# Program order for half 1's first product, a block sum behind two low parts, output-block differences in place, and the last bank in two halves

## The chip, the cores and the metric

The kernel runs on one core of one Trainium2 chip. The metric is the device time of the whole program in microseconds, the median over the runs shown. Engines are named as the profile names them: PE is TensorE's matmul stream, PEld its weight loads, DVE is VectorE, ACT is ScalarE, POOL is GpSimd and SP is SyncE, which here only issues DMAs.

## What is computed

One hybrid encoder layer on 1024 tokens of width 1024, in float32:

```
mod = silu(c) @ w_ada + b_ada;  sh1, sc1, gt1, sh2, sc2, gt2 = split(mod, 6)
h = rmsnorm(x, norm1_g) * (1 + sc1) + sh1
u, v, q, k, va, gate_a, gate_b = split(h @ w_in)
a_out = gmlp_branch(u, v, ...) @ w_a
b_out = window_attention_branch(q, k, va, ...) @ w_b
x = x + gt1 * ((sigmoid(gate_a) * a_out + sigmoid(gate_b) * b_out) @ w_o)
h2 = rmsnorm(x, norm2_g) * (1 + sc2) + sh2
f_gate, f_up = split(h2 @ w_ffn_in)              # two times 1024 x 2816
x = x + gt2 * ((silu(f_gate) * f_up) @ w_ffn_out)
```

## The kernel before

**Precision and units.** Every float32 matrix is used as a rounded high part and a low part (value minus high part), and every product is three matmuls: high by high, high by low, low by high. A *unit* is a 128x1024 piece of a weight: `unit` (line 157) takes its raw load (SP queue, tag `raw`, three buffers), a cast on ACT for the high part (tag `wh`, three buffers) and a subtraction on DVE, or on POOL, for the low part (tag `wl`, three buffers).

**Halves.** `half(hf)` (line 747) does the first sub-layer's projections and both branches for 512 tokens, first for half 0, then for half 1. Its first product is the loop `for k in range(KT)`, line 897: eight steps, and in each step the 128 rows k of h meet the q weights (four 512-wide outputs) and the k/v weights (in half 1, three 256-wide outputs). A q unit serves two steps and a k/v unit four. In half 1 the loop also emits, at steps 1, 3 and 5, the unit of the q weights for the next two steps; at step 3 the raw load of the second k/v unit and at step 4 that unit; after steps 2 and 3 the loads of two columns of `w_ada` (`ada_half_load`, tags `hs` and `xs`, two buffers each); after steps 4 and 5 the two dot products on DVE of a column loaded earlier (`ada_half`), followed by the loads of another column into the same two buffers; after steps 6 and 7 only the dot products. The v product (`v_product`, line 1004) follows, with units of `w_v`.

**What sets the order.** Instructions of one engine run in the order of its queue. A planner writes that order from its own estimate of when inputs are ready, except where an instruction is pinned. With `in_order[0]` set, each instruction of DVE, ACT, POOL and PE is queued behind the instruction emitted before it on its engine. Loads through `load` (line 137) are always pinned so on SP. Half 0's first product runs with `in_order` set and half 1's does not. `after(ins, prev)` (line 143) pins one instruction behind one other. The second sub-layer runs under a manual schedule: program order throughout.

**Block sums.** From the end of half 1 on, products are done as seven-product (Strassen-like) block products, which need sums of blocks. `block_load(k, "b1")` (line 596) makes one of their inputs, the sum of the high and low part of a block of half 1's h, on POOL. At the same time POOL subtracts the low parts of the units of `w_ab` for the branch projections (`prepare`, line 1020, called with POOL by default).

**The FFN.** For each of 22 feature tiles f there are seven steps i of 12 matmuls (`product`, `evict`). Two neighbouring tiles make a pair e = f // 2, whose four 512-wide results are the blocks b0 to b3 of one tile `o` of the pool `mid` (eight buffers). `hidden_sums` (line 1681) stores `o` to `tA[e]` by a POOL DMA and queues four DVE operations in the list `later`, one of which is run at each step: d0 = b0-b1, d1 = -d0-b3, d2 = b3-b1, d3 = -d1-b2. They are written to a second `mid` tile `n`, which is stored to `tB[e]`. The first one is queued at step 3 of the pair's second tile, the other three at that tile's step 6. `load_out` and `out_sums` use `mid` too (`wo`), with a store to `wS`. The blocks of T3 and T4 and the sums `ws` hold five of the eight buffers.

**The output product.** 77 work items (seven products by eleven pairs) of 12 matmuls each run from `wS`, `tA`, `tB` and `w_out` (`step_mm`, line 2018). The last two items are done together, one 512-wide bank d of four after another; `finish` scales a bank on DVE, adds it into `acc` and stores it by an SP DMA.

Of the kernel before, what the change touches and what calls it, by code (L numbers as in the profile page):

```python
# [8 lines left out]
F32 = mybir.dt.float32  # L9
# [3 lines left out]
ALU = mybir.AluOpType  # L13
# [3 lines left out]
P = 128  # L17
# [3 lines left out]
HALF = 512  # L21
# [17 lines left out]
def kernel(  # L39
# [25 lines left out]
    in_order = [False]  # L65
# [18 lines left out]
    V, A, G, T = (Engine(e) for e in (nc.vector, nc.scalar, nc.gpsimd, nc.tensor))  # L84
# [16 lines left out]
    def nm(s):  # L101
        n_names[0] += 1
        return f"{s}_{n_names[0]}"
# [48 lines left out]
    def raw_unit(src):  # L152
        r = wpool.tile([P, UNIT], F32, tag="raw", name=nm("raw"))
        load(r, src)
        return r

    def unit(src, eng=None, raw=None):
        r = raw if raw is not None else raw_unit(src)
        h = wpool.tile([P, UNIT], F32R, tag="wh", name=nm("wh"))
        l = wpool.tile([P, UNIT], F32R, tag="wl", name=nm("wl"))  # L160
        A.copy(h, r)
        (eng or V).tensor_tensor(l, r, h.bitcast(F32), op=ALU.subtract)
        return h, l

    def mm3(out, a, b, first, last):
# [73 lines left out]
    NP = NF // 2  # L239
# [351 lines left out]
    nsh, g1b = nshb[:, :8], nshb[:, 8:]  # L591
    blk = {}

    chunk, kinds = {}, []

    def block_load(k, name):
        if k < 4:
            if name == "b1":
                chunk[name] = stream("xs")
                G.tensor_tensor(chunk[name], *(x[:, k, :].bitcast(F32) for x in blk["B22"]), op=ALU.add)  # L600
                return
            chunk[name] = stream("hs" if name[0] == "a" else "xs")
            store(chunk[name], (x0d if name[0] == "a" else x1sd)[4 * int(name[1]) + k])
# [143 lines left out]
    def half(hf):  # L747
# [142 lines left out]
        def halo_product(k):  # L890
            w = kv_unit(k // 4)
            ok = slice(k % 4 * 256, k % 4 * 256 + 256)
            for a, b in ((k, 0), (k, 1), (KT + k, 0)):
                T.matmul(kps[NT], hl4[:, a, :], w[b][:, ok], start=k + b == 0 and a == 0,
                         stop=a == 2 * KT - 1)

        for k in range(KT):
            if hf == 0:
                x = xt[k]
# [120 lines left out]
        def prepare(eng=G):  # L1020
            if srcs:
                units.append(unit(srcs.pop(0), eng))

        def begin_unit():
            r = raw_unit(srcs.pop(0))
# [518 lines left out]
    def pool_dma(dst, src):  # L1544
        nc.gpsimd.dma_start(dst, src)

    def dma(dst, src):
        nc.sync.dma_start(dst, src)
# [127 lines left out]
            if later:  # L1676
                later.pop(0)()

    first_sum = {}

    def hidden_sums(f):

        e, t = divmod(f, 2)
        if t == 0:
            hidden[e].append(mid.tile([P, 2048], F32, tag="mid", name=nm("hid")))
        o, n = hidden[e]
        b = [o[:, i * Q : (i + 1) * Q] for i in range(4)]
        d = [n[:, i * Q : (i + 1) * Q] for i in range(4)]
        if t == 0:
            first_sum[e] = lambda: V.tensor_tensor(d[0], b[0], b[1], op=ALU.subtract)  # L1690
            return
        pool_dma(tA[e], o)
        later.append(lambda: V.scalar_tensor_tensor(out=d[1], in0=d[0], scalar=-1.0, in1=b[3],
                                                    op0=ALU.mult, op1=ALU.subtract))
        later.append(lambda: V.tensor_tensor(d[2], b[3], b[1], op=ALU.subtract))
        later.append(lambda: (V.scalar_tensor_tensor(out=d[3], in0=d[1], scalar=-1.0, in1=b[2],
                                                     op0=ALU.mult, op1=ALU.subtract),
                              pool_dma(tB[e], n)))

    wo_raw = {}  # L1700

# [103 lines left out]
    def out_row(e, t, d):  # L1805
        return w_out[2 * e + t][:, d * Q : (d + 1) * Q]

    def blk(x, i):
        return lambda e: x[e][:, i * Q : (i + 1) * Q]
# [2 lines left out]
    OUT = (  # L1812
        (lambda e: out_row(e, 0, 0), blk(tA, 0), 1, True),
        (lambda e: out_row(e, 1, 0), blk(tA, 2), 1, False),
        (blk(wS, 1), blk(tB, 2), 0, True),
        (lambda e: out_row(e, 1, 1), blk(tB, 3), 0, False),
        (blk(wS, 3), blk(tB, 0), 1, True),
        (blk(wS, 0), blk(tB, 1), 1, False),
        (blk(wS, 2), blk(tA, 3), 1, False),
    )  # L1820
    work = [(i, e) for i in range(7) for e in range(NP)]
# [14 lines left out]
    def split_step(n):  # L1836
        if n < len(work):
            if n % 5 < 3:
                ready[n] = wtiles()
            else:  # L1840
                ready[n] = [outp[0].tile([P, UNIT], F32R, tag=f"o{x}", name=nm(f"o{x}"), bufs=2)
                            for x in "hl"]
            split2(raws[n], *ready[n])
# [9 lines left out]
    with tc.manual_schedule():  # L1853
# [46 lines left out]
        for f, i in steps:  # L1900
            product(f, i)
            if chain:
                run_chain(2 if (f, i) < (0, 5) else 0)
            u = place[f, STEPS[i][0]]
            copies = f and i in (0, 2, 3) or f < 2 and i in (4, 5)
            if copies:
                evict(f, i)
            prepare(u + 2, 1)
            if chain:
                run_chain(2 if (f, i) != (0, 5) else 0)  # L1910
            if i == 6 or f < EARLY:
                prepare(u + 2, 1)
            if not copies:
                evict(f, i)
            if (f, i) == (0, 5):
                evict(0, 6)
            if i == 3 and f % 2:
                later.append(first_sum.pop(f // 2))
            if i == 6 or (f, i) == (0, 5):
                hidden_sums(f)  # L1920
            elif f > 2:
                run_later(1)
            if f >= EARLY:
                e, p = divmod(7 * (f - EARLY) + i, 10)
                if e < NP and p == 0:
                    load_out(e)
                if e < NP and p == 5:
                    later.extend(lambda e=e, p=p: out_sums(e, p) for p in range(4))
            if (f, i) == (NF - 3, 0):
                again.extend(stream("hs") for _ in range(2))  # L1930
                for j in range(2):
                    dma(again[j], silu_d[:, j * 512 : (j + 1) * 512])
            if (f, i) == (NF - 2, 6):
                row_load(0)
            if f == NF - 1 and i in (3, 5):
                split_step(i // 2 - 1)
# [16 lines left out]
        def put(q, hf, d):  # L1953
            (dma if (q, hf) == (0, 1) else pool_dma)(
                outT[(4 * q + d) * P : (4 * q + d + 1) * P, hf * HALF : (hf + 1) * HALF],
                acc[q][hf][:, d, :])

        def finish(i, d, bank):
            gt = mod[:, GT2 + d : GT2 + d + 1]
            if i == 0:  # L1960
                A.copy(c1[:, d, :], bank)
            elif i == 1:
                o = acc[0][0][:, d, :]
                V.scalar_tensor_tensor(out=o, in0=bank, scalar=gt, in1=o, op0=ALU.mult, op1=ALU.add)
                put(0, 0, d)
            elif i == 2:
                V.tensor_tensor(e7[:, d, :], bank, c1[:, d, :], op=ALU.add)
            elif i == 3:
                V.tensor_tensor(e4[:, d, :], bank, c1[:, d, :], op=ALU.add)
            elif i == 4:  # L1970
                V.tensor_tensor(e4[:, d, :], e4[:, d, :], bank, op=ALU.subtract)
            elif i == 5:
                last5[d] = tmp()
                A.copy(last5[d], bank)
            else:
                o = acc[0][1][:, d, :]
                V.scalar_tensor_tensor(out=o, in0=bank, scalar=gt, in1=o, op0=ALU.mult, op1=ALU.add)
                put(0, 1, d)
# [36 lines left out]
            if n == 54:  # L2015
                V.tensor_scalar(ngt, mod[:, GT2 + 4 : GT2 + 8], -1.0, None, op0=ALU.mult)

        def step_mm(n, d):
            i, e = work[n]
            _, _, b, first = OUT[i]  # L2020
            w = ready[n]
            ds, ts = slice(d * P, (d + 1) * P), slice(Q, 2 * Q)
            for j, (p, q) in enumerate(((0, 0), (0, 1), (1, 0))):
                T.matmul(sets[b][d], w[p][:, ds], w[q][:, ts], start=first and e + j == 0,
                         stop=e == NP - 1 and j == 2, skip_group_check=True)

        sets = {}
        for n, (i, e) in enumerate(work):
            _, _, b, first = OUT[i]
            if e == 0 and first:  # L2030
                sets[b] = [at_bank() if b else mm_bank() for _ in range(4)]
            last = n == len(work) - 1
            if n < len(work) - 2:
                for d in range(4):
                    step_mm(n, d)
            elif last:
                for d in range(4):
                    for m in (n - 1, n):
                        step_mm(m, d)
            if e == NP - 1:  # L2040
                for d in range(4):
                    finish(i, d, sets[b][d])
            split_step(n + 4)
            fetch(n + 12)
            gain_dots(n)
            if n in (8, 24, 40, 52):
                m = (8, 24, 40, 52).index(n)
                load_acc(m // 2, m % 2)
            if e < 4:
                finish_rest(i - 1, e)  # L2050
            if i == 6 and 4 <= e < 8:
                second_row(e - 4)
# [68 lines left out]
```

## Time and profile before

| | us |
|---|---|
| median of 3 runs | 1237.61 |
| lowest and highest run | 1235.74, 1238.73 |
| the profiled execution's own time | 1236.14 |
| its span, first to last instruction | 1234.4 |
| PE busy within the span | 1225.4 (99%) |
| DVE, ACT, POOL busy | 907.8, 582.6, 181.0 |

Matmul ends are modelled, so PE's busy time contains pipelined overlap, and a short stall can hide in it: the start-to-start distance of neighbouring matmuls is the better measure. All engine instructions carry line 77, since a wrapper records them, so groups are told apart by tile names. A wait is put down to the one releaser that came last.

### The profile page before, as it was taken

To read this page: it belongs to the slowest core of one execution; us is meant where nothing else is said; L and a number is where in the kernel's file an instruction comes from. 1 tells how busy PE (TensorE), PEld (TensorE's weight loads), DVE (VectorE), ACT (ScalarE), POOL (GpSimd) and SP (SyncE) were. 2 spreads that over 40 slices of the span, in tenths; PEclk is the share of its full clock that TensorE was granted. 3 is DMA by queue.
4 is the path that set the end of the run, shared out by engine and by line. 5 is a ranking of instruction groups with operands and counts; after the bars stand their busy time and mean duration, and the time that the engine had idled before them with its cause. 6 is when DMAs were issued, how large, how long until landed. Compare 5 with 4: busy or idle time off the path is not lost.

```text
span 1234.4 us, 15751 instructions
## 1 busy us (share of the span) xinstructions
PE 1225.4 (99%) x5679; PEld 1018.8 (83%) x5679; DVE 907.8 (74%) x1535; ACT 582.6 (47%) x951; POOL 181.0 (15%) x228
## 2 busy tenths in 40 slices
PE   9999999999999999999999999999999999999998
PEld 7888888888888888888888888888888888888887
DVE  7897884487898799977797766666766667666746
ACT  5667864267877324534453333333333334434342
POOL 0123420023442011222100000010000000010001
PEclk8999999999999999999999999999999999999999
DMA  9732158431157467878413535455554459996552
GB/s 330 278 103 88 67 189 301 143 101 52 57 167 247 162 208 240 281 277 265 177 35 121 185 143 200 158 195 200 185 202 169 170 188 380 329 360 226 188 171 102
DMA packets 78528, 235.77 MB, mean 191 GB/s; under 512 B 9457, under 2 KB 9457, under 8 KB 73458
## 3 DMA queue, kind: packets, MB, share of 16 engines
q1 hardware_dynamic: 56018, 141.43, 33.0%
q0 software_dynamic: 18976, 87.04, 19.8%
q10 hardware_dynamic: 3456, 6.29, 1.4%
q8 instruction: 44, 0.72, 0.2%
q14 instruction: 34, 0.28, 0.1%
HBM read 177.06 MB, written 57.67 MB: 190 GB/s over the span
## 4 chain that ended last, share of the span: by engine, by line
PE 78%; DVE 7%; issue 5%; ACT 5%; DMA 3%; POOL 1%; SPq 0%; ACTq 0%; DVEq 0%; POOLq 0%
PE at L77 42%; PE mm L77 37%; DVE wl L77 2%; DVE mid L77 2%; ACT wh L77 1%; ACT mid L77 1%; DVE xs L77 1%; ACT lb L77 1%; ACT pH L77 1%; DMA hs<-in_w_ada_dram 1%; DVE ws L77 1%; DVE hid L77 1%; DMA wS<-wo 0%; DMA x1sd<-xs 0%; DMA xs<-x1sd 0%
## 5 line engine op out<-in xcount | busy, mean ns | idle before, releaser
L77 ACT CAST wh<-raw 128x1024 fp32r<-128x1024 f32 (+1 forms) x154 | 160.8, 1046 | 139.9 <-PE at L77 37.3
L77 PE MATMUL mm<-mid,wh 128*128 128x512 f32 x696 | 214.9, 390 | 0.5 <-DVE xs L77 0.3
L77 DVE TENSOR_TENSOR wl<-raw,wh 128x1024 fp32r<-128x1024 f32 (+1 forms) x140 | 169.3, 1213 | 61.5 <-ACT wh L77 61.0
L77 PEld LDWEIGHTS mm<-mid,wh 128*128 128x128 f32 x696 | 130.3, 188 | 28.3 <-DVE xs L77 1.3
L77 PE MATMUL at<-j,wh 128*128 128x512 f32 x464 | 142.9, 389 | 0.0
L77 PE MATMUL mm<-mid,wl 128*128 128x512 f32 x348 | 135.5, 389 | 0.6 <-POOL wl L77 0.6
L77 PE MATMUL mm<-wh,h 128*128 128x512 f32 x384 | 129.1, 398 | 1.0 <-ACT h L77 0.9
L77 PEld LDWEIGHTS at<-j,wh 128*128 128x128 f32 x464 | 87.0, 188 | 18.3 <-ACT xs L77 0.2
L77 DVE TENSOR_TENSOR wl<-ws,wh 128x1024 fp32r<-128x1024 f32 (+1 forms) x55 | 62.0, 1128 | 46.0 <-ACT wh L77 46.0
L77 PE MATMUL at<-j,wl 128*128 128x512 f32 x232 | 90.4, 390 | 0.1
L77 PE MATMUL at<-h,wh 128*128 128x512 f32 x288 | 88.9, 390 | 0.0
L77 PE MATMUL mm<-j,wh 128*128 128x512 f32 x288 | 88.9, 390 | 0.0
L77 PE MATMUL mm<-h,wh 128*128 128x512 f32 x272 | 84.6, 392 | 0.0
L77 PEld LDWEIGHTS mm<-wh,h 128*128 128x128 f32 x384 | 71.1, 188 | 15.7 <-ACT h L77 1.8
L77 ACT CAST wh<-ws 128x1024 fp32r<-128x1024 f32 (+1 forms) x55 | 53.5, 972 | 61.2 <-DVE ws L77 43.4
L77 PEld LDWEIGHTS mm<-mid,wl 128*128 128x128 f32 x348 | 65.3, 188 | 14.6 <-POOL wl L77 1.0
L77 PE MATMUL mm<-wl,h 128*128 128x512 f32 x192 | 75.2, 392 | 0.4 <-DVE wl L77 0.4
L77 PEld LDWEIGHTS at<-h,wh 128*128 128x128 f32 x288 | 53.9, 188 | 11.1
L77 PEld LDWEIGHTS mm<-j,wh 128*128 128x128 f32 x288 | 53.9, 188 | 11.1
L77 DVE TENSOR_TENSOR ol<-raw,oh 128x1024 fp32r<-128x1024 f32 x30 | 36.6, 1222 | 31.6 <-ACT oh L77 30.0
L77 ACT ACTIVATE xs<-xs 128x512 f32<-128x512 f32 x21 | 13.3, 633 | 98.0 <-DVE xs L77 98.0
L77 PEld LDWEIGHTS mm<-h,wh 128*128 128x128 f32 x272 | 50.6, 188 | 10.4
(300 smaller groups left out, 2580.0 us busy)
## 6 DMA issues: line engine op xcount, KB each, us to landing
raw<-in_w_gate_dram SPq DMA_DIRECT2D x28, 512.0 KB, 5.1
tA<-hid POOLq DMA_DIRECT2D x11, 1024.0 KB, 4.9
tB<-hid POOLq DMA_DIRECT2D x11, 1024.0 KB, 5.1
wo<-in_w_out_dram POOLq DMA_DIRECT2D x22, 512.0 KB, 6.3
wS<-wo POOLq DMA_DIRECT2D x11, 1024.0 KB, 5.4
raw<-wS SPq DMA_DIRECT2D x44, 256.0 KB, 3.5
raw<-tB SPq DMA_DIRECT2D x44, 256.0 KB, 4.3
raw<-in_w_out_dram SPq DMA_DIRECT2D x33, 256.0 KB, 5.1
```

Source lines behind the costliest of these rows:

```text
L77: ins = f(*args, **kw)
```

## The change

There are four edits.

- `in_order[0] = True` stands ahead of the loop of the first product, so that half 1's loop is pinned in program order on PE, ACT, DVE and POOL too. After the loop it is cleared, as before.
- The POOL sum for `b1` is pinned behind the POOL low part of the last unit made by `prepare`, the second one of `w_ab`.
- The differences d0 to d3 are written over the blocks of `o` (for all pairs but the last, which keeps a second tile), in the order d0, d2, d1, d3 and at the places 0, 1, 3, 2. They are queued at step 3 of the next pair's first tile, and no first sum is queued ahead of the pair's store any more. `OUT` takes the blocks of `tB` from their new places.
- In the last two work items, bank 3 is computed and finished in two 256-wide halves: six matmuls for each half, then two scale-and-add operations and two stores.

```diff
+    unit_low = [None]
...
-        (eng or V).tensor_tensor(l, r, h.bitcast(F32), op=ALU.subtract)
+        unit_low[0] = (eng or V).tensor_tensor(l, r, h.bitcast(F32), op=ALU.subtract)
...
-                G.tensor_tensor(chunk[name], *(x[:, k, :].bitcast(F32) for x in blk["B22"]), op=ALU.add)
+                after(G.tensor_tensor(chunk[name], *(x[:, k, :].bitcast(F32) for x in blk["B22"]),
+                                      op=ALU.add), low_of[0])
...
+        in_order[0] = True
         for k in range(KT):
...
                 units.append(unit(srcs.pop(0), eng))
+                low_of[0] = unit_low[0]
...
         if t == 0:
-            hidden[e].append(mid.tile([P, 2048], F32, tag="mid", name=nm("hid")))
-        o, n = hidden[e]
...
-        if t == 0:
-            first_sum[e] = lambda: V.tensor_tensor(d[0], b[0], b[1], op=ALU.subtract)
             return
+        o = hidden[e][0]
         pool_dma(tA[e], o)
...
+        n = o if e < NP - 1 else mid.tile([P, 2048], F32, tag="mid", name=nm("hid"))
+        b0, b1, b2, b3 = (o[:, i * Q : (i + 1) * Q] for i in range(4))
+        d0, d2, d3, d1 = (n[:, i * Q : (i + 1) * Q] for i in range(4))
...
+        block_sum[e] = [
+            lambda: V.tensor_tensor(d0, b0, b1, op=ALU.subtract),
+            lambda: V.tensor_tensor(d2, b3, b1, op=ALU.subtract),
+            lambda: negated(d1, d0, b3),
+            lambda: (negated(d3, d1, b2), pool_dma(tB[e], n)),
+        ]
+        if e == NP - 1:
+            later.extend(block_sum.pop(e))
...
-            if i == 3 and f % 2:
-                later.append(first_sum.pop(f // 2))
+            if i == 3 and f % 2 == 0 and f:
+                later.extend(block_sum.pop(f // 2 - 1))
...
+        def finish_last(bank, half):
+            o = acc[0][1][:, 3, half]
+            V.scalar_tensor_tensor(out=o, in0=bank[:, half], scalar=mod[:, GT2 + 3 : GT2 + 4], in1=o,
+                                   op0=ALU.mult, op1=ALU.add)
+            dma(outT[3 * P : 4 * P, HALF + half.start : HALF + half.stop], o)
...
             elif last:
-                for d in range(4):
+                for d in range(3):
                     for m in (n - 1, n):
                         step_mm(m, d)
+                halves = [slice(h * 256, h * 256 + 256) for h in range(2)]
+                for half in halves:
+                    for m in (n - 1, n):
+                        step_mm(m, 3, half)
...
+                if last:
+                    for half in halves:
+                        finish_last(sets[b][3], half)
```

More of the change, by code (lines that the diff above doesn't have):

```diff
@@ L592 @@
     blk = {}
-    chunk, kinds = {}, []
+    chunk, kinds, low_of = {}, [], [None]
     def block_load(k, name):
@@ L1677, in run_later @@
                 later.pop(0)()
-    first_sum = {}
+    block_sum = {}
     def hidden_sums(f):
@@ L1684, in hidden_sums, with negated @@
         if t == 0:
-            hidden[e].append(mid.tile([P, 2048], F32, tag="mid", name=nm("hid")))
-        o, n = hidden[e]
-        b = [o[:, i * Q : (i + 1) * Q] for i in range(4)]
-        d = [n[:, i * Q : (i + 1) * Q] for i in range(4)]
-        if t == 0:
-            first_sum[e] = lambda: V.tensor_tensor(d[0], b[0], b[1], op=ALU.subtract)
             return
+        o = hidden[e][0]
         pool_dma(tA[e], o)
[L1693 to L1698, printed above, removed]
+        n = o if e < NP - 1 else mid.tile([P, 2048], F32, tag="mid", name=nm("hid"))
+        b0, b1, b2, b3 = (o[:, i * Q : (i + 1) * Q] for i in range(4))
+        d0, d2, d3, d1 = (n[:, i * Q : (i + 1) * Q] for i in range(4))
+        def negated(out, x, y):
+            V.scalar_tensor_tensor(out=out, in0=x, scalar=-1.0, in1=y, op0=ALU.mult,
+                                   op1=ALU.subtract)
+        block_sum[e] = [
[6 more added lines that the diff above has]
+            later.extend(block_sum.pop(e))
     wo_raw = {}
@@ L1814 @@
         (lambda e: out_row(e, 1, 0), blk(tA, 2), 1, False),
-        (blk(wS, 1), blk(tB, 2), 0, True),
-        (lambda e: out_row(e, 1, 1), blk(tB, 3), 0, False),
+        (blk(wS, 1), blk(tB, 1), 0, True),
+        (lambda e: out_row(e, 1, 1), blk(tB, 2), 0, False),
         (blk(wS, 3), blk(tB, 0), 1, True),
-        (blk(wS, 0), blk(tB, 1), 1, False),
+        (blk(wS, 0), blk(tB, 3), 1, False),
         (blk(wS, 2), blk(tA, 3), 1, False),
@@ L2016, in gain_dots, with step_mm @@
                 V.tensor_scalar(ngt, mod[:, GT2 + 4 : GT2 + 8], -1.0, None, op0=ALU.mult)
-        def step_mm(n, d):
+        def step_mm(n, d, half=slice(0, Q)):
             i, e = work[n]
@@ L2021, in step_mm @@
             w = ready[n]
-            ds, ts = slice(d * P, (d + 1) * P), slice(Q, 2 * Q)
+            ds, ts = slice(d * P, (d + 1) * P), slice(Q + half.start, Q + half.stop)
             for j, (p, q) in enumerate(((0, 0), (0, 1), (1, 0))):
-                T.matmul(sets[b][d], w[p][:, ds], w[q][:, ts], start=first and e + j == 0,
+                T.matmul(sets[b][d][:, half], w[p][:, ds], w[q][:, ts], start=first and e + j == 0,
                          stop=e == NP - 1 and j == 2, skip_group_check=True)
@@ L2036 @@
             elif last:
-                for d in range(4):
+                for d in range(3):
                     for m in (n - 1, n):
                         step_mm(m, d)
+                halves = [slice(h * 256, h * 256 + 256) for h in range(2)]
+                for half in halves:
+                    for m in (n - 1, n):
+                        step_mm(m, 3, half)
             if e == NP - 1:
-                for d in range(4):
+                for d in range(3 if last else 4):
                     finish(i, d, sets[b][d])
+                if last:
+                    for half in halves:
+                        finish_last(sets[b][3], half)
             split_step(n + 4)
```

## The prediction

> **What bounds the kernel now.** I read the page first, then the waits with the engine set to PE.
>
> ```profile
> span 1234.4 us, 15751 instructions
> PE 1225.4 (99%) x5679; PEld 1018.8 (83%) x5679; DVE 907.8 (74%) x1535; ACT 582.6 (47%) x951; POOL 181.0 (15%) x228
> ```
> ```profile
> PE mm L77 <- POOL wl L77: 0.6, 1, 0.6
> PE mm L77 <- DVE wl L77: 0.4, 1, 0.4
> ```
>
> PE is the bound: 1234.4 - 1225.4 = 9.0 us of idle time are in the whole span. No edit removes a 512-wide product, so a gain can only be a stall of PE that goes, or a shorter tail. The two waits are single events. I looked for their places, and for further short ones, in the timeline of PE:
>
> ```profile
> 216.84 0.39 PE L77 MATMUL mm<-wl,h 128*128 128x512 f32 x1
> 217.07 0.28 PE L77 MATMUL at<-wh,h 128*128 128x256 f32 x1
> ...
> 217.66 0.28 PE L77 MATMUL at<-wl,h 128*128 128x256 f32 x1
> ...
> 219.06 0.40 PE L77 MATMUL mm<-wh,h 128*128 128x512 f32 x1
> 219.85 0.50 PE L77 MATMUL mm<-wl,h 128*128 128x512 f32 x1 [0.39 <-DVE wl L77]
> ...
> 348.97 0.50 PE L77 MATMUL mm<-mid,wl 128*128 128x512 f32 x1 [0.55 <-POOL wl L77]
> ```
>
> A 512-wide matmul lasts 0.39 us but the next starts 0.23 us after it (216.84 to 217.07), so an idle gap g costs g + 0.16: 0.55 us at 219.85 (half 1's first product) and 0.71 at 348.97 (the first branch projection). The FFN's stalls I read from windows:
>
> ```profile
> 680.00:700.00 20.00, 19.86 (x88) 16.14 (x87) 15.22 (x23) 5.74 (x9) 1.07 (x2) 1.00 0.51 183
> 920.00:940.00 20.00, 19.68 (x87) 15.97 (x86) 15.45 (x22) 6.47 (x9) 2.13 (x4) 1.00 0.46 163
> 940.00:960.00 20.00, 19.92 (x89) 16.16 (x87) 13.59 (x20) 6.38 (x9) 1.07 (x2) 1.00 0.61 207
> ```
>
> The second number is PE's busy time; all other 20 us windows of the FFN after 700 have 20.00. Idle 0.14, 0.32 and 0.08, so 0.30 + 0.48 + 0.24 = 1.02 us. In all 0.55 + 0.71 + 1.02 = 2.28 us are there to be won, less than 0.2% of 1237.61 (2.48 us, about what a measurement of this kernel can tell from no change).
>
> **Edit 1, program order.** Why was the low part late at 219.85?
>
> ```profile
> 217.96 0.69 DVE L77 SCALAR_TENSOR_TENSOR xs<-xs,silu_c 128x512 f32<-128x512 f32 x1 [5.17 <-DMA xs<-in_w_ada_dram]
> ...
> 218.57 1.22 DVE L77 TENSOR_TENSOR wl<-raw,wh 128x1024 fp32r<-128x1024 f32 x1
> ...
> 228.31 2.36 DVE L77 TENSOR_TENSOR wl<-raw,wh 128x1024 fp32r<-128x1024 f32 x2 [0.79 <-ACT wh L77]
> ```
>
> The planner queued a dot product ahead of it, and DVE sat 5.17 us for that dot's load. In program order all dots stand behind the low parts of steps 1, 3 and 4, so this stall goes: -0.55. But each dot also frees the buffer of the next `w_ada` load on SP:
>
> ```profile
> 214.19 1.01 SPq L138 DMA_DIRECT2D hs<-in_w_ada_dram  x2
> 219.82 0.33 SPq L138 DMA_DIRECT2D raw<-in_w_q_dram  x1
> 220.19 2.10 SPq L138 DMA_DIRECT2D xs<-in_w_ada_dram  x2
> ```
>
> SP's order does not change: the two `hs` loads of step 4, then the raw load of the last q unit, then two `xs` loads of step 5, then `w_v`. Before, the `hs` buffers came free early and the q load left at 219.82. Now the dots of step 4 are pinned behind the low part of step 4's k/v unit. That unit cannot start before step 3 is over, since it needs a buffer that PE reads until then:
>
> ```profile
> 227.23 2.00 ACT L77 CAST wh<-raw 128x1024 fp32r<-128x1024 f32 x2 [7.27 <-PE mm L77]
> ```
> ```profile
> 227.38 0.40 PE L77 MATMUL mm<-wh,h 128*128 128x512 f32 x1
> ...
> 235.06 0.40 PE L77 MATMUL mm<-wh,h 128*128 128x512 f32 x1
> ...
> 242.70 0.40 PE L77 MATMUL mm<-wh,h 128*128 128x512 f32 x1
> ```
> ```profile
> raw<-in_w_v_dram SPq DMA_DIRECT2D x4, 512.0 KB, 3.6
> raw<-in_w_q_dram SPq DMA_DIRECT2D x3, 512.0 KB, 4.3
> ```
>
> These are the starts of steps 4 and 6 and of the v product. On before's clock: cast from 227.23, low part from 228.31 to 229.5 (half of the 2.36), two dots of about 0.65 to 230.8, the second `hs` issue (half of 1.01) to 231.3, then the q load. It takes 3.6 to 4.3, I take 4.0 with the `hs` loads just ahead: 235.3. Cast 1.05 (half of 2.00, rounded up) to 236.35, low part 1.2 to 237.55. Step 6 wants the high part at 235.06 and the low part 0.23 later: PE gets its second matmul at 237.55 instead of 235.29, a stall of 2.26, call it 2.2, with one matmul in its middle. With the load at 3.6 it is 1.9; if the three loads (1 MB) go at the pace of 4.3 each half, about 4.
>
> The Trainium skill, DMA: Bandwidth & Descriptors, section Anatomy of one DMA, gives about 2.0 us fixed plus bytes over 436 GB/s, which I estimate at 3.2 us for this load; that was fitted on GpSimd's path, the rows above are slower, and by it the stall would be 1.5.
>
> The same happens once more, with more cover. The dots of step 5 stand behind that low part: 238.85, the `xs` issues to 239.3, then `w_v`'s first load: 243.3, cast 244.35, low part 245.55. The v product starts at 242.70 + 2.2 = 244.9 and wants the low part 0.23 later: 0.4. The copies that empty the old banks are pinned behind that low part on DVE, which may add some tenths; I take 0.6 in all, between 0 and 1.5. Edit 1: -0.55 + 2.2 + 0.6 = +2.25, from +1 to +5 if the chain holds.
>
> **Edit 2, the block sum.**
>
> ```profile
> 345.28 1.30 POOL L77 TENSOR_TENSOR xs<-h,h 128x512 f32<-128x512 f32 x1
> 346.53 4.76 POOL L77 TENSOR_TENSOR wl<-raw,wh 128x1024 fp32r<-128x1024 f32 x2
> ```
> ```profile
> 355.70 0.68 DVE L77 TENSOR_TENSOR xs<-xs,xs 128x512 f32<-128x512 f32 x1
> ```
>
> Without the 1.30 ahead of them the two low parts run from 345.28, the first to 347.65. PE wants it at 348.26 (348.97 less 0.71), so the stall goes, -0.71, with 0.6 to spare. The sum then runs from 350.0 to 351.3; its reader on DVE starts at 355.70, so 4.4 us cover it. POOL has nothing else queued there. ACT's negations of the same block must now follow the sum. If the planner queues them too early, ACT waits up to 4.7 us with casts behind it: 0 to +1; I take 0.
>
> **Edit 3, in place.** The operations stay four per pair at 0.6 to 0.7 us. What goes is the second tile:
>
> ```profile
> 919.27 0.69 DVE L77 TENSOR_TENSOR hid<-hid 128x512 f32<-128x512 f32 x1 [5.60 <-DMA wS<-wo]
> ...
> 943.25 0.69 DVE L77 TENSOR_TENSOR hid<-hid 128x512 f32<-128x512 f32 x1 [3.29 <-DMA wS<-wo]
> ```
>
> There the first difference waits for a `wS` store to free a buffer, and the evictions and low parts behind it on DVE reach PE late. Counting buffers in program order, three of eight are free for `o` and `wo`; without `n`, each new `o` gets one whose last store was issued at least three steps (8.2 us) earlier, so DVE does not wait. In place, d0 must wait until the store to `tA` has read the tile; it comes at least four steps, 12 x 0.227 x 4 = 10.9 us, after the store's place.
>
> ```profile
> tA<-hid POOLq DMA_DIRECT2D x11, 1024.0 KB, 4.9
> ```
>
> So that is covered, by 6 us. The stall at 698 lies in a crowded DVE stretch where two differences run just ahead of the eviction; now one does, 0.6 us less against 0.30. All three go: -1.02. But the last pair, which had one of its four differences done beforehand, now runs all four behind the final evictions, ahead of the low part of output item 2:
>
> ```profile
> 1024.45 0.68 DVE L77 SCALAR_TENSOR_TENSOR hid<-hid,hid 128x512 f32<-128x512 f32 x1
> 1025.05 1.22 DVE L77 TENSOR_TENSOR wl<-raw,wh 128x1024 fp32r<-128x1024 f32 x1
> ```
> ```profile
> 1026.64 0.39 PE L77 MATMUL at<-wl,wh 128*128 128x512 f32 x1
> ```
>
> It ends at 1026.27 and PE wants it at 1026.64. One more 0.6 (1024.45 to 1025.05) makes it 1026.9: a stall of 0.3. Edit 3: -0.7, from -1.0 to 0.
>
> **Edit 4, the last bank.**
>
> ```profile
> 1230.19 0.39 PE L77 MATMUL at<-wh,wl 128*128 128x512 f32 x1
> 1230.61 0.75 DVE L77 SCALAR_TENSOR_TENSOR mid<-at,mod,mid 128x512 f32<-128x512 f32 x1 [0.61 <-PE at L77]
> ```
> ```profile
> 343.95 1.27 DVE L77 SCALAR_TENSOR_TENSOR mid<-at,cc,mid 128x256 f32<-128x256 f32 x3 [1.23 <-PE at L77]
> ```
> ```profile
> out_dram<-mid SPq DMA_DIRECT2D x4, 256.0 KB, 2.0
> ```
>
> A 256-wide matmul takes 0.118 ((217.66 - 217.07) / 5), so twelve cost 1.42 against 6 x 0.227 = 1.36: +0.06. Whether the first half is scaled while PE fills the second decides the rest. Both halves lie in one bank, and both finishes are emitted behind all matmuls. If they wait, two 256-wide operations of 0.42 (1.27 / 3) end 0.1 later than one of 0.75, and the last store is half as long, of 2.0 in all: about -0.1 net. If not: -0.5. I take -0.1, from -0.5 to +0.2.
>
> **Sum.** +2.25 - 0.71 - 0.7 - 0.1 = +0.7 us. The profiled execution took 1236.14, 1.5 below the median of 1237.61; I add the difference to the median: 1238.3.
>
> **Rivals.** *The q load comes in time.* If the dots get ahead, or the loads land much sooner, edit 1 is -0.55 and the sum -0.55 - 0.71 - 0.7 - 0.1 = -2.1: 1235.5. Against it: dots, SP's order and the busy buffer are three fixed links, and even a load of 3.0 leaves 1.3 us. Chance 0.18.
>
> *The clock falls in the stall: slower.* The granted clock is the number behind POOL's:
>
> ```profile
> 8.00:12.00 4.00, 4.00 (x21) 3.74 (x20) 2.59 (x5) 2.85 (x5) 0.00 (x0) 0.58 1.03 360
> 16.00:18.00 2.00, 2.00 (x9) 1.90 (x9) 0.52 (x1) 0.00 (x0) 0.00 (x0) 0.50 1.05 423
> ```
>
> Near the start, after a broken stretch, it is halved. A half clock for t us costs t / 2. If it falls at step 6 and stays low as long as that stretch, some 10 us, the price is 5 us: 1238.3 + 5 = 1243.3; at 3.4 us low it is 1240. It decides from a stall in which PE is idle for most of a few microseconds; 2.2 us, split in two, is near that. Chance 0.17. TensorE: Matmul & The Clock Gate in the Trainium skill, Part 1, says half rate follows at least one idle window of about 3.4 us; by that 2.2 us is too short.
>
> *The stalls only move.* Pinning shifts the planner's order elsewhere in half 1, and new short waits eat what edits 2 and 3 save, or edit 1's chain costs less: 1237.6, within 1 us. Chance 0.13.
>
> **Numbers.** My forecast has 0.52, with its own range from 1237.0 to 1240.5. The range of 8 in 10 is 1235.4 to 1241.0: it takes in the first and third rival and the clock's cheap end. Below 1235.1 only the first rival's lower edge lies: 0.05. Above 1240.1 lie the second rival and the forecast's upper tail: 0.26. Same: 0.69.
>
> **What would show it.** Right: no wait at the second q unit's low part (219.85 before); the `hs` loads of step 4 leaving behind that step's k/v low part, and a PE wait on `wh`, then `wl`, at step 6; no PE wait on POOL's low part; no DVE wait on `wS<-wo`; a PE stall of about 0.3 at output item 2; two 256-wide finishes, both after the last matmul. Wrong: step 6 starting without a wait, or a granted clock below 1.00 after it.

## The result, and the profile after

Over six runs the changed kernel takes 1243.9 us in the median (1242.11 to 1245.32), the kernel before 1237.07, also over six. The ratio is 1.0054 with a 95% interval of 1.0043 to 1.0064: slower by 6.7 us (5.3 to 7.9), where the forecast was 1238.3 with a range that ended at 1241.0. The profiled execution took 1243.97 us, 7.8 above the one shown of before.

The first lines of the page of after, to be read against the first fence of the prediction:

```profile
span 1242.2 us, 15761 instructions
PE 1227.1 (99%) x5685; PEld 1018.9 (82%) x5685; DVE 909.3 (73%) x1536; ACT 582.3 (47%) x951; POOL 180.8 (15%) x228
```

PE has 1.7 us more busy time and 6.1 us more idle time (15.1 against 9.0). The waits of PE in after (us in total, times, longest) say where to look:

```profile
PE mm L77 <- DVE xs L77: 2.2, 1, 2.2
PE mm L77 <- ACT wh L77: 1.9, 1, 1.9
PE mm L77 <- DVE wl L77: 1.8, 4, 0.8
...
PE mm L77 <- ACT mid L77: 1.2, 1, 1.2
```

The wait on POOL's low part (0.6 in before) is gone, as forecast. None of these four had this size in before; the first was not forecast at all.

**Half 1's first product.** The timelines of after, of DVE, SP, ACT and PE in turn, over steps 4 to 6 and the v product:

```profile
226.69 1.23 DVE L77 TENSOR_TENSOR wl<-raw,wh 128x1024 fp32r<-128x1024 f32 x1 [6.41 <-ACT wh L77]
227.83 0.68 DVE L77 SCALAR_TENSOR_TENSOR hs<-hs,silu_c 128x512 f32<-128x512 f32 x1
...
235.47 1.23 DVE L77 TENSOR_TENSOR wl<-raw,wh 128x1024 fp32r<-128x1024 f32 x1 [5.90 <-ACT wh L77]
```
```profile
228.55 0.94 SPq L138 DMA_DIRECT2D hs<-in_w_ada_dram  x2
229.58 0.38 SPq L138 DMA_DIRECT2D raw<-in_w_q_dram  x1
237.34 0.94 SPq L138 DMA_DIRECT2D xs<-in_w_ada_dram  x2
238.37 8.35 SPq L138 DMA_DIRECT2D raw<-in_w_v_dram  x4
```
```profile
234.40 1.04 ACT L77 CAST wh<-raw 128x1024 fp32r<-128x1024 f32 x1 [7.74 <-DMA raw<-in_w_q_dram]
244.05 1.05 ACT L77 CAST wh<-raw 128x1024 fp32r<-128x1024 f32 x1 [8.61 <-DMA raw<-in_w_v_dram]
```
```profile
235.49 0.49 PE L77 MATMUL mm<-wh,h 128*128 128x512 f32 x1 [1.94 <-ACT wh L77]
236.75 0.50 PE L77 MATMUL mm<-wl,h 128*128 128x512 f32 x1 [0.77 <-DVE wl L77]
245.64 0.50 PE L77 MATMUL mm<-wh,h 128*128 128x512 f32 x1 [1.19 <-ACT mid L77]
246.41 0.50 PE L77 MATMUL mm<-wl,h 128*128 128x512 f32 x1 [0.28 <-DVE wl L77]
```

This is the forecast chain, link by link: low part at 226.69, dots behind it, `hs` loads, q load at 229.58, cast at 234.40, low part at 235.47, PE at 236.75. The first gap of each place costs 0.16 us more than its bracket (2.10 and 1.35 us); the second I take from the starts, less the usual 0.23 (236.75 - 235.49 gives 1.03, 246.41 - 245.64 gives 0.55). So step 6 stalls by 2.10 + 1.03 = 3.13 us and the v product by 1.35 + 0.55 = 1.90. At the v product the first gap ends with ACT's copy that empties a bank; that copy stands behind the late cast of 244.05, and the second gap ends with the low part, so the load sets the sum of the two.

**The FFN.** The timelines of POOL, DVE and PE of after, around the first difference of pair 1:

```profile
696.31 0.53 POOL L1550 DMA_DIRECT2D tA<-hid  x1 [4.28 <-DVE hid L77]
```
```profile
697.26 0.69 DVE L77 TENSOR_TENSOR wl<-ws,wh 128x512 fp32r<-128x512 f32 x1 [1.25 <-ACT wh L77]
700.65 0.69 DVE L77 TENSOR_TENSOR hid<-hid 128x512 f32<-128x512 f32 x1 [2.69 <-DMA tA<-hid]
...
704.93 0.68 DVE L77 TENSOR_TENSOR xs<-mm,xs 128x512 f32<-128x512 f32 x1
```
```profile
703.08 0.39 PE L77 MATMUL at<-j,wl 128*128 128x512 f32 x1
705.67 1.20 PE L77 MATMUL mm<-mid,wh 128*128 128x512 f32 x2 [2.20 <-DVE xs L77]
```

The store of pair 1 to `tA` leaves at 696.31. DVE reaches the difference that overwrites its source right behind the low part, at 697.95, and waits 2.69 us for the store's end. The eviction of the next bank (704.93) stands behind it in DVE's queue, and PE waits for that bank: the stall is 2.36 us, at the place where before had 0.30 (698.65). The waits of DVE's differences on stores in the whole trace, first in before, then in after:

```profile
DVE hid L77 <- DMA wS<-wo: 17.5, 6, 5.6
```
```profile
DVE hid L77 <- DMA tA<-hid: 2.7, 1, 2.7
```

The waits on `wS` are gone, as forecast, and the other nine pairs that are done in place wait for no store. Then comes a second loss. In the windows of after, the number behind POOL's is the granted clock:

```profile
702.31:705.72 3.41, 1.21 (x7) 0.67 (x5) 2.29 (x4) 1.05 (x1) 0.00 (x0) 1.00 0.00 0
705.72:709.13 3.41, 3.41 (x8) 2.74 (x9) 2.90 (x5) 1.03 (x2) 0.00 (x0) 0.50 0.00 0
```

Behind the stall the clock is 0.50 for 3.41 us: eight matmuls in that time instead of fifteen, 1.7 us lost.

**The rest.** Two places in the gate stage (block products behind half 1, near 399 and 405 us) have 0.76 us more stall than before (below, edit 2). Some further stalls of tenths between 470 and 490 us lie where other executions of kernels with the same code there have none, or others. The FFN stalls of before near 922 and 945 us are gone, output item 2 stalls by 0.29, and the tail is 0.2 shorter.

### The profile page after: what moved, and what is told of

Same layout as the page of the kernel before. It is cut to its first block, busy times and chain, and to the rows that moved or that the text cites. A ratio compares the mean times of both kernels' runs of the same rounds, so it can differ in the third digit from the quotient of the medians.

```text
span 1242.2 us, 15761 instructions
## 1 busy us (share of the span) xinstructions
PE 1227.1 (99%) x5685; PEld 1018.9 (82%) x5685; DVE 909.3 (73%) x1536; ACT 582.3 (47%) x951; POOL 180.8 (15%) x228
## 4 chain that ended last, share of the span: by engine, by line
PE 79%; DVE 8%; DMA 5%; issue 4%; ACT 3%; POOL 0%; SPq 0%; DVEq 0%; ACTq 0%; POOLq 0%
PE at L77 40%; PE mm L77 38%; DVE mid L77 2%; DVE wl L77 2%; ACT wh L77 2%; DMA hs<-in_w_ada_dram 1%; DMA raw<-in_w_ga_dram 1%; ACT mid L77 1%; DVE hs L77 1%; DVE xs L77 1%; DMA raw<-in_w_gb_dram 1%; DVE t L77 1%; DMA xs<-x1sd 0%; DMA raw<-in_w_v_dram 0%; ACT t L77 0%
## 5 line engine op out<-in xcount | busy, mean ns | idle before, releaser
L77 ACT CAST wh<-ws 128x1024 fp32r<-128x1024 f32 (+1 forms) x55 | 53.5, 972 | 58.6 <-DVE ws L77 40.4
L77 PE MATMUL mm<-j,wl 128*128 128x512 f32 x144 | 56.2, 390 | 0.5 <-DVE wl L77 0.5
```

The lines of the kernel that those rows point to most:

```text
L77: ins = f(*args, **kw)
```

## The experiments

### Without edit 1 (a_no_order)

```diff
-        in_order[0] = True
         for k in range(KT):
```

> The changed kernel with half 1 left to the planner, as before; edits 2 to 4 stay. My theory: edit 1 is the larger part of the loss. Its stalls in the trace of after are 3.13 us at step 6 and 1.90 at the v product, +0.2 at step 0, less the 0.56 that it removes, about +4.7; without it the time falls from 1243.9 to about 1239.2. Rival: the loss lies elsewhere (edit 3's stall at tile 4, with the half clock behind it, and 2 us in the gate stage); then it falls by less than 2.5, to 1241.5 or above. Also watched: whether the 2 us that the gate stage lost go with edit 1.

Measured: 1238.76 us, ratio to before 1.0019 (1.0009 to 1.0029), against 1.0054 with edit 1: 4.3 us less. The stalls at step 6 and at the v product are not in its trace. Edit 1 is the larger part of the loss, and 2.3 us stay without it. The gate stage's stalls between 470 and 490 us are absent too, although its code there is that of after: they vary from one execution to the next. Those near 394 and 400 us stay, so they are not edit 1's.

### Edit 1 alone (b_order)

```diff
+        in_order[0] = True
         for k in range(KT):
```

> The kernel before with edit 1 alone: half 1 in program order. My theory: +4.7 us, about 1241.8, with PE stalls at step 6 and at the v product. If the gate stage's 2 us come from the shifted order too, 1243.8. My prediction's sum for this edit was +2.25: 1239.3. Rival: +1 or less.

Measured: 1240.85, ratio 1.0040 (1.0028 to 1.0053), +4.9 us. From the other side the same size, and twice what the prediction summed. Its trace has the two stalls (2.88 and 1.60 us).

### Edit 3 alone (b_inplace)

```diff
-            hidden[e].append(mid.tile([P, 2048], F32, tag="mid", name=nm("hid")))
...
+        n = o if e < NP - 1 else mid.tile([P, 2048], F32, tag="mid", name=nm("hid"))
...
-            if i == 3 and f % 2:
-                later.append(first_sum.pop(f // 2))
+            if i == 3 and f % 2 == 0 and f:
+                later.extend(block_sum.pop(f // 2 - 1))
```

> The kernel before with edit 3 alone: the differences in place. My theory: pair 1's first difference waits on its store two steps after the store's place, PE stalls by some 2.3 us at tile 4 and the granted clock is halved for 3.4 us behind it (+1.7); less 1.1 of the other stalls, plus 0.3 at the output, about +3.4: 1240.5. If the clock does not fall, +1.7: 1238.8. By the prediction's step (four steps of cover) it is -0.7: 1236.4.

Measured: 1239.08, ratio 1.0011 (0.9998 to 1.0023), +1.4 us: the step's -0.7 would be 0.9994, below the interval, and the trace has a stall of 2.30 us at tile 4 with the half clock behind it. But it is less than my +3.4, and no change is just inside the interval. Its runs spread from 1235.35 to 1241.07, and the profiled one is the longest. That the half clock came in some of them only is possible, since the windows further down show that it depends on where the stall falls, but it isn't shown: the other runs have no trace, and before, without that stall, spreads as far (1233.25 to 1241.73 over 34 runs).

### Edit 2 alone (b_sum)

```diff
-                G.tensor_tensor(chunk[name], *(x[:, k, :].bitcast(F32) for x in blk["B22"]), op=ALU.add)
+                after(G.tensor_tensor(chunk[name], *(x[:, k, :].bitcast(F32) for x in blk["B22"]),
+                                      op=ALU.add), low_of[0])
```

> The kernel before with edit 2 alone: the block sum behind the low parts on GpSimd. My theory and the prediction: the 0.72 us stall of the first branch projection goes, -0.7: 1236.4. Rival: the gate stage's later small stalls (about 2 us in after, near 399, 405, 471 and 473 us) are this edit's own; then +1.3: 1238.4, and they show in its trace.

Measured: 1237.52, ratio 0.9997 (0.9984 to 1.0010): nothing that can be told from no change. The trace says why. PE in b_sum, then the same matmul in before:

```profile
347.89 0.40 PE L77 MATMUL mm<-mid,wl 128*128 128x512 f32 x1
...
394.81 0.50 PE L77 MATMUL mm<-j,wl 128*128 128x512 f32 x1 [0.47 <-DVE wl L77]
```
```profile
395.35 0.39 PE L77 MATMUL mm<-j,wl 128*128 128x512 f32 x1
```

The first projection no longer waits, but 47 us later a stall of 0.63 us stands where before had none. DVE in b_sum, then in before, for the low part that it waits for:

```profile
393.53 1.23 DVE L77 TENSOR_TENSOR wl<-raw,wh 128x1024 fp32r<-128x1024 f32 x1 [0.26 <-ACT wh L77]
```
```profile
393.91 1.23 DVE L77 TENSOR_TENSOR wl<-raw,wh 128x1024 fp32r<-128x1024 f32 x1 [0.26 <-ACT wh L77]
```

PE comes to this place 1.2 us earlier on its own clock (394.18 without the stall, against 395.35), the low part only 0.38 us earlier. DVE, which makes it, has little room in between: it is busy for 40.4 of the 45 us from 350 to 395 us in before. The rival's "later small stalls" are this edit's at this one place; those between 470 and 490 us are not in this trace.

### The q load issued early (a_early_load)

```diff
-                    wq_next = unit(w_q[(k + 1) // 2], V)
+                    wq_next = unit(w_q[(k + 1) // 2], V, wq_raw if k == 5 else None)
                 if k == 3:
                     wk_raw = raw_unit(w_kv[1])
+                    wq_raw = raw_unit(w_q[3])
```

> The changed kernel with one issue moved: the raw load of the last q unit stands in SP's queue at step 3, ahead of the w_ada loads that wait for the dots, instead of behind them at step 5. Program order stays. My theory: the stalls at step 6 (3.13 us in after) and at the v product (1.90) come from that load's late issue, behind dots that are pinned behind a low part; both go, and the time falls from 1243.9 to about 1239, as without edit 1 (1238.8). Rival: the low part is late because of its own place on DVE, whatever the load; then step 6 still stalls by 2 us or more and the time stays above 1241.5.

Measured: 1237.98, ratio 1.0009 (0.9997 to 1.0021): 5.6 us below after, no more than without edit 1 (1.0019). SP in this kernel:

```profile
212.58 0.33 SPq L138 DMA_DIRECT2D raw<-in_w_q_dram  x1
213.00 0.88 SPq L138 DMA_DIRECT2D xs<-in_w_ada_dram  x2
228.64 0.94 SPq L138 DMA_DIRECT2D hs<-in_w_ada_dram  x2
```

The q load leaves at 212.58 instead of 229.58; its cast runs right behind step 4's and its low part right behind that step's dots, and PE waits neither at step 6 nor at the v product. The low part's place on DVE is unchanged, so the rival falls: it was the load's place in SP's queue.

### A second tile for pair 1 (a_pair1_tile)

```diff
-        n = o if e < NP - 1 else mid.tile([P, 2048], F32, tag="mid", name=nm("hid"))
+        n = o if e not in (1, NP - 1) else mid.tile([P, 2048], F32, tag="mid", name=nm("hid"))
```

> The changed kernel, but pair 1 (and the last, as in the change) writes its differences to a second tile, so that its first difference needs no store to finish; the other pairs stay in place. My theory: the 2.36 us stall at tile 4 goes, and with it the half clock behind it (1.7 where it came), against 0.3 that stays there: 1243.9 - 2.1 to 1243.9 - 3.8, so 1240.1 to 1241.8. Rival: the wait is one for a free buffer and not for the store, or the second tile brings such a wait: the stall at tile 4 stays near 2 us and the time at 1243.

Measured: 1240.02, ratio 1.0022 (1.0012 to 1.0032), 3.9 us below after. DVE no longer waits at the first difference of pair 1, which stands right behind a low part as in after:

```profile
694.90 0.69 DVE L77 TENSOR_TENSOR wl<-ws,wh 128x512 fp32r<-128x512 f32 x1 [1.25 <-ACT wh L77]
695.51 0.68 DVE L77 TENSOR_TENSOR hid<-hid 128x512 f32<-128x512 f32 x1
```

No stall is left at tile 4, not even the 0.3 that I allowed. The second tile found a buffer without a wait. This execution has a half clock too, but at step 6 (below).

### Pair 1's differences one step earlier (a_pair1_sooner)

```diff
-            if i == 3 and f % 2 == 0 and f:
+            if i == (2 if f == 4 else 3) and f % 2 == 0 and f:
```

> The changed kernel with pair 1's differences queued one step (2.7 us) earlier, one step behind the store instead of two. My theory: DVE waits for the end of the same store, so the wait grows from 2.69 to about 5.4 us, but the evictions that stood ahead of it now stand behind it: the PE stall at tile 4 is 2 to 5 us, and the granted clock is halved behind it, since more than half of one 3.41 us window is idle. Rival: the wait is not for the store; then it stays at 2.7 us and only moves.

Measured: one run, 1246.58 us, so its time says little. DVE in this kernel:

```profile
701.08 1.42 DVE L77 TENSOR_TENSOR hid<-hid 128x512 f32<-128x512 f32 x2 [2.77 <-DMA tA<-hid]
```

My wait of 5.4 us was wrong: on DVE nothing stands between the two places, so the wait is 2.77 us, as the rival had it. But the wait is for the store: it ends 4.42 us after the store's issue (696.66), as in after (696.31 to 700.65, 4.34). The second difference now also stands ahead of the eviction; PE stalls by 3.16 us, and the clock is halved for two windows instead of one.

### Both mends (a_both)

The diffs of the early q load and of pair 1's second tile together.

> Both mends on the changed kernel: the early q load and pair 1's second tile. My theory: the two losses are separate and add: 1243.9 - 4.9 - 2.1 to 3.8, so 1235.2 to 1236.9, level with before or up to 1.5 us faster. Rival: what remains of the edits (the saved stalls come back in the gate stage, near 395 and 401 us) costs more than it brings; then 1238 or above.

Measured: 1234.90, ratio 0.9985 (0.9971 to 1.0000), 1.8 us below before, with no change at the edge of the interval, and 8.5 below after (9.0 by the medians). That is just past the fast end of my range. Within the intervals the two losses add, and together they account for all of the slowdown.

### Both mends without edit 2 (both_no_sum)

```diff
-                after(G.tensor_tensor(chunk[name], *(x[:, k, :].bitcast(F32) for x in blk["B22"]),
-                                      op=ALU.add), low_of[0])
+                G.tensor_tensor(chunk[name], *(x[:, k, :].bitcast(F32) for x in blk["B22"]), op=ALU.add)
```

> The kernel with both mends, with edit 2 undone: the block sum stands ahead of the low parts on GpSimd again. My theory: the stall that edit 2 removes at the first branch projection (0.72 us) comes back, and the one that every trace with edit 2 shows some 46 us later (0.4 to 0.7 at the first products on the block's j chunks) shrinks by as much, since DVE's and ACT's chain of block work sets that place; the time stays within 0.5 us of the kernel with both mends. Rival, the prediction's sum: edit 2 is worth 0.71, and the time rises by 0.7.

Measured: 1235.00, ratio 0.9987 (0.9977 to 0.9997), 0.1 us from the kernel with edit 2; the intervals are too wide to tell 0.7 from 0 by themselves. PE in both_no_sum, then in a_both:

```profile
347.20 0.50 PE L77 MATMUL mm<-mid,wl 128*128 128x512 f32 x1 [0.57 <-POOL wl L77]
```
```profile
392.91 0.73 PE L77 MATMUL mm<-j,wh 128*128 128x512 f32 x2 [0.27 <-ACT wh L77]
394.17 0.50 PE L77 MATMUL mm<-j,wl 128*128 128x512 f32 x1 [0.53 <-DVE wl L77]
```

The stall of 0.74 us at 347 comes back and the two of 0.43 and 0.70 at 393 and 394 vanish. All eight traces with edit 2 have a stall of 0.32 to 0.70 at that matmul; of the six without it, five have none and one, of edit 4 alone, 0.26.

### The last pair's first difference early (all_mends)

```diff
+            if e == NP - 1:
+                last_diff.append(mid.tile([P, 2048], F32, tag="mid", name=nm("hid")))
...
+            if i == 3 and f == NF - 1:
+                o, n = hidden[NP - 1][0], last_diff[0]
+                later.append(lambda: V.tensor_tensor(n[:, :Q], o[:, :Q], o[:, Q : 2 * Q],
+                                                     op=ALU.subtract))
```

> The kernel with both mends, and the last pair's first difference queued a step ahead of its last tile's end, as before, into a second tile. My theory: the 0.29 us stall at output item 2 goes, nothing else moves: 0.3 us below the kernel with both mends, too little for the comparison to tell, but its trace shows it. Rival: the second tile, taken earlier, waits for a buffer and a stall of 0.2 to 0.5 appears at the last pair's first tile.

Measured: 1234.44, ratio 0.9984 (0.9970 to 0.9998). The place on DVE in after, where two subtractions run behind the last eviction, and in all_mends, where one does:

```profile
1030.51 1.28 DVE L77 TENSOR_TENSOR hid<-hid 128x512 f32<-128x512 f32 x2
1031.72 1.41 DVE L77 SCALAR_TENSOR_TENSOR hid<-hid,hid 128x512 f32<-128x512 f32 x2
1033.04 1.22 DVE L77 TENSOR_TENSOR wl<-raw,wh 128x1024 fp32r<-128x1024 f32 x1
```
```profile
1024.01 0.69 DVE L77 TENSOR_TENSOR hid<-hid 128x512 f32<-128x512 f32 x1
1024.62 1.41 DVE L77 SCALAR_TENSOR_TENSOR hid<-hid,hid 128x512 f32<-128x512 f32 x2
1025.95 1.22 DVE L77 TENSOR_TENSOR wl<-raw,wh 128x1024 fp32r<-128x1024 f32 x1
```

The stall at output item 2 is gone and no wait for a buffer appears. It is the fastest median of all, but 0.46 us from a_both is inside the scatter. The trace also has a stall of 0.99 us at 553 us, where no other trace has one; the edit comes more than 400 us behind that place, so I count it as scatter.

### Edit 1 alone with the early load (b_order_early)

The first lines of edit 1 and the diff of the early q load, on the kernel before.

> The kernel before with program order (edit 1) and the last q unit's raw load issued at step 3. My theory: what edit 1 alone cost (4.9 us in the comparison) was that load's place; with the load early, program order is worth the stall of the low part at step 2 (0.55 in the trace of before, up to 1.4 in other profiled executions): 0.4 to 1.2 us faster than before. Rival: pinning the dots costs elsewhere too; then level with before or slower.

Measured: 1236.41, ratio 1.0003 (0.9993 to 1.0014). The 4.6 us between this and edit 1 alone are the load's place. That program order itself gains 0.4 to 1.2 us isn't borne out: the point is +0.4 and the interval takes in a gain of 0.9. Its trace lacks the stall at step 2, but has 0.20 at step 0 and the usual scatter later on.

### Edit 4 alone (b_last)

```diff
+                halves = [slice(h * 256, h * 256 + 256) for h in range(2)]
+                for half in halves:
+                    for m in (n - 1, n):
+                        step_mm(m, 3, half)
...
+                    for half in halves:
+                        finish_last(sets[b][3], half)
```

> The kernel before with edit 4 alone: the last bank in two halves. My theory and the prediction: both finishes wait for the last matmul, some 0.1 us less tail, no difference that the comparison can tell. Rival: the first half's finish runs beside the second half's matmuls; then the span from the last matmul's start to the end falls by 0.5 or more.

Measured: 1237.14, ratio 1.0006 (0.9996 to 1.0017). DVE in b_last:

```profile
1232.23 0.88 DVE L77 SCALAR_TENSOR_TENSOR mid<-at,mod,mid 128x256 f32<-128x256 f32 x2 [0.68 <-PE at L77]
```

Its last matmul starts at 1231.91: both finishes come behind it. From that start to the span's end it is 4.0 us, against 4.2 in before, as expected; the rival's 0.5 isn't there.

## Why the prediction was wrong

The forecast was +0.7; measured is +6.7 by the ratio. Every sign that the prediction named as right is in the trace of after, and none of them looks at an early pair's store. Of the 6.0 us that are missing, edit 1 has 2.1 to 2.7, edit 2 about 0.7 and edit 3 the rest, some 3. By the prediction's own steps:

**Edit 1: mechanism right, two terms too small.** All links hold. From the cast of step 4's unit to the q load's issue the prediction had 231.3 - 227.23 = 4.1 us; after has 229.58 - 225.60 = 4.0. The mis-sized term is the load: "I take 4.0", and it took 4.82 (229.58 to 234.40), so step 6 stalls by 3.13 instead of 2.2. The same term for `w_v` took 5.68 (238.37 to 244.05), so the v product stalls by 1.90 instead of 0.6. The medians of before, 3.6 and 4.3, were of loads in other company; here two `w_ada` loads of 256 KB leave within 1.1 us ahead of each, and two more `w_v` loads within 1 us behind the second. In before the first `w_v` load leaves more than 6 us behind the last `w_ada` load and lands in 3.4 us. In a_early_load the q load, with two `w_ada` loads behind it instead of ahead, lands in 3.8. So the company fits as the cause, but no run changes it alone. The Trainium skill's figure (DMA: Bandwidth & Descriptors, section Anatomy of one DMA), from which I estimated 3.2 us, is further off. Edit 1 came to +4.3 to +4.9 by the ratios, at the upper end of "from +1 to +5".

**Edit 2: right at its place, wrong in the sum.** The stall of 0.71 went as worked out, with the cover named. What is late next, once the stall is gone, was not asked: the next low part that PE needs in time had 0.2 us of slack in before (393.91 + 1.23 = 395.14, against 395.35), and it moved by 0.38 us where PE moved by 1.2. In the traces the net is about 0 (0.72 won, 0.63 lost in b_sum); the comparisons alone can't tell 0 from -0.7.

**Edit 3: the failed step.** "In place, d0 must wait until the store to `tA` has read the tile; it comes at least four steps, 12 x 0.227 x 4 = 10.9 us, after the store's place ... So that is covered, by 6 us." Four steps hold for tiles with seven steps. Tiles below `EARLY` (6), whose first two steps run ahead of this loop, start at step 2, as the list of steps (line 1791 of the kernel before) says, so pair 1's difference comes two steps behind its store, and since the store waits for the last eviction, DVE gets there 1.64 us after the store's issue. The store takes 4.34. So the term "-1.02" was wrong in one of its three places: the stall near 698 us, counted as -0.30, grew from 0.30 to 2.36 and brought 1.7 of half clock. The rest was right: the stalls near 922 and 945 us are gone, and output item 2 stalls by 0.29, forecast 0.3. In the trace of after edit 3 comes to 2.36 - 0.30 - 0.72 + 0.29 + 1.7 = +3.3, where the forecast was -0.7. Giving this one pair a second tile is worth 3 to 4 us (1.0054 to 1.0022; 1.0009 to 0.9985). By edit 3 alone (+1.4, against -0.7) the pair costs 2.1; the intervals are too wide to tell these sizes apart.

**Edit 4: right**, -0.2 in the trace, nothing in the ratio.

**The clock.** The second rival came true, but at another place: not at step 6 of after, whose stall is the longer one (3.13), but behind the FFN's 2.36. The trace's clock record of after changes at 9.40, 16.23, 705.72 and 709.13 us, and (705.72 - 16.23) / 3.413 = 202.0: changes lie on a grid of 3.413 us. On that grid the windows tell the two stalls apart. After at step 6, then a_no_order, b_inplace and a_pair1_tile, each with the window that follows:

```profile
234.68:238.09 3.41, 1.83 (x7) 1.30 (x8) 2.58 (x6) 0.76 (x1) 0.00 (x0) 1.00 0.01 2
238.09:241.51 3.42, 3.42 (x21) 3.00 (x20) 2.53 (x10) 0.00 (x0) 0.00 (x0) 1.00 0.86 223
```
```profile
695.44:698.85 3.41, 1.74 (x8) 1.12 (x6) 2.26 (x4) 1.05 (x1) 0.00 (x0) 1.00 0.00 1
698.85:702.27 3.42, 2.95 (x13) 2.44 (x14) 3.42 (x6) 0.63 (x1) 0.00 (x0) 1.00 0.00 0
```
```profile
700.62:704.03 3.41, 1.42 (x6) 1.20 (x7) 3.30 (x5) 0.32 (x2) 0.00 (x0) 1.00 0.00 0
704.03:707.45 3.42, 3.42 (x10) 2.65 (x9) 2.23 (x4) 1.43 (x2) 0.00 (x0) 0.50 0.19 54
```
```profile
232.40:235.82 3.42, 1.14 (x6) 0.57 (x4) 0.94 (x1) 1.04 (x1) 0.00 (x0) 1.00 0.12 48
235.82:239.23 3.41, 3.06 (x7) 2.48 (x8) 3.27 (x13) 0.00 (x0) 0.00 (x0) 0.50 0.29 99
```

In these stretches, PE busy for 1.74 us or more of a window: the clock stays. PE busy for 1.42 or less: the next window is halved. The step-6 stall of after straddles two windows, that of a_pair1_tile falls mostly into one. So the FFN stall costs 2.3 us (a_no_order) or 4.0 (after) by chance of phase, and that after has the half clock at tile 4 and not at step 6 is luck too. The prediction's rival looked for "a stall in which PE is idle for most of a few microseconds", which is near. By the page of the Trainium skill named there (TensorE: Matmul & The Clock Gate, Part 1), a whole idle window of about 3.4 us is needed. In these traces 2.0 us of idle time in one window (3.41 - 1.42) was enough. The start of the kernel doesn't fit a rule by busy time alone: there the clock of all fourteen traces is halved for two or three windows, though PE counts as busy for 3.07 of 3.41 us in the window ahead of it in after. Why stays open.

**The chances.** The own range ended at 1240.5 because edit 3's range stopped at 0: its cover had been worked out for the late tiles alone, and no bound was set for the case that it fails.

## What to carry to other kernels

When an operation is made to overwrite the source of a store, check the distance for every iteration, the short first ones above all, and give a cover that isn't proved a price and a bound. When work is pinned, follow each DMA issue that the pinned work releases: here one raw load moved two steps up in SP's queue gave back all that program order had cost. A saved stall counts only as far as the next supply that doesn't move with the bound engine has slack.

## What the runs showed of the hardware

In these traces the clock changes on a fixed grid of 3.413 us: in the eight windows with the longest stalls, in seven kernels, PE busy for 1.74, 1.78 and 1.83 us kept it at 1.00, and 1.42, 1.32, 1.29, 1.21 and 1.14 gave 0.50 for the next 3.41 us. The half clock at the start of the kernel, behind windows in which PE counts as busy, isn't covered by this. A second half-rate window followed in a_pair1_sooner, where PE was busy for 2.53 of 3.41 us at half rate. And the casts that waited for a 512 KB load behind 512 KB of other loads on the same queue started 4.82 and 5.68 us after its issue, where the medians of before to landing are 3.6 and 4.3.
